# Chunked attention: softmax reciprocals transposed by TensorE, returned through DRAM and applied by GpSimd, and row statistics placed after three projections

## The chip, the cores and the metric

The kernel runs on one core of one Trainium2 chip. The metric is the device time of one execution in microseconds (us); the median of several executions is compared. A trace of one profiled execution shows when each engine worked: TensorE (PE, with its weight loads PEld), VectorE (DVE), ScalarE (ACT), GpSimd (POOL), and SyncE (SP), whose queue issues most DMA transfers.

## The reference

Two layers over 1024 tokens of width 1024: an even one (two recurrent head groups) and an odd one (softmax attention of 64-token chunks), each followed by a squared-ReLU MLP and a gated embedding. The change lies in the odd layer's attention: 16 heads of width 64, each chunk against itself and the eight chunks before it.

```python
def rmsnorm(x, g, eps=NORM_EPS):
    xf = x.astype(jnp.float32)
    y = xf * lax.rsqrt(jnp.mean(xf * xf, -1, keepdims=True) + eps)
    return (y * g.astype(jnp.float32)).astype(x.dtype)
...
def chunk_band_attention(h, w_qkv, q_g, k_g, rel_bias):
    qkv = (h @ w_qkv).reshape(bsz, seq, 3, C_HEADS, C_HEAD_DIM)
    q = rmsnorm(qkv[:, :, 0], q_g) * (C_HEAD_DIM ** -0.5)
    k = rmsnorm(qkv[:, :, 1], k_g)
    v = qkv[:, :, 2]
...
        s = jnp.einsum('bqhd,bkhd->bhqk', q_c, k_b).astype(jnp.float32) + bias
        s = jnp.where(valid, s, -jnp.inf)
        prob = jax.nn.softmax(s, -1).astype(v.dtype)
        return jnp.einsum('bhqk,bkhd->bqhd', prob, v_b)
...
        h = rmsnorm(x, norm_mix_g[i])
            mix = chunk_band_attention(h, attn_w_qkv[o], attn_q_g[o], attn_k_g[o], attn_rel_bias[o]) @ attn_w_out[o]
        x = x + mix
```

## The kernel before

The program is generated for one core. Activations lie transposed (128 features by 1024 tokens, in two halves `hf` of 512). Float32 products are made of two-part splits: a rounded high part and the remainder, three matmuls for each product (`xh*wh`, `xh*wl`, `xl*wh`). All matmuls are issued by the helper `mm` (L177), all transposes by TensorE by `tr` (L192), and most splits by `split_scaled` (L349 on ScalarE, L350 on VectorE); so these lines of the profile hold many tiles, and the tile names tell them apart.

**Steps.** Attention runs over 16 steps `s`: 8 pairs of heads (`pr`) times 2 halves of the tokens (`hf`). Four kinds of generators ("lanes") write the instructions down, and `run` (L130) merges them by a planner's clock: each `yield` names a duration in the table `LAT` after which the lane may go on, or a mark of another lane that it has to see first.

- `attn_in` (L1828) projects q, k and v of one step: four blocks `i` of 128 tokens, 24 matmuls each, into a PSUM bank `dps` (two banks in turn, `bank`). ScalarE evicts with the row statistics `rscol` as a scale (L1861 to `qk`, L1865 to `vs`), VectorE writes the remainder (L1866). GpSimd squares q and k (L1873, tile `sq`), VectorE sums the squares (L1874, `ss`), takes a reciprocal root and scales `qk` (L1877). The lane may be three steps ahead of attention. In the first block (L1858) `row_stats` (L366) sums the squares of layer 0's output over the features with matmuls against ones, and VectorE makes `rscol` of them. Those squares are summed by GpSimd while layer 0 ends (L1627, tile `acc`).
- `attn_norm` (L1880) transposes q and k on TensorE and splits them (tiles `F`, `Ql`).
- `attn_lane` (L1807), two of them, takes the 64 jobs (step, head, half of the half) in turn and runs `attn_block` (L1907). A job has two rows of 128 queries. Scores go to the banks `sn` (the last three key blocks, which have a bias) and `sf` (the far ones); VectorE adds the bias `toep` and takes the maximum (L1957, L1965); ScalarE takes the exponential and the row sums (L1967, L1970), VectorE adds the sums and takes the reciprocal (L1972, L1973), and ScalarE scales the whole row of probabilities `pb` by it (L1974). Then TensorE transposes the probabilities (bank `pt`, two in turn), they are split to `ptile` (L349, L350), and TensorE multiplies them with the values into the bank `po`. When both halves are done, ScalarE and VectorE add the two parts to `y` (L2015, L2016), and SP stores `y` to DRAM (L2022, `yd`). The last step keeps `y` on the chip.

After the last step of `attn_ins`, the same lane projects the layer's embedding (L1650, with sums of squares on GpSimd at L1675) and begins the output projection (`out_early`, L1679), which reads `yd` back.

**What sets the order.** Beyond the lanes, a scheduler orders the instructions that are ready, engine by engine. Each engine executes its list strictly in order: what stands behind a waiting instruction waits too. SP's list has the loads of weights (L1823), of biases (L1841) and the stores of `y`.

Of the kernel before, what the change touches and what calls it, by code (L numbers as in the profile page):

```python
# [8 lines left out]
F32 = mybir.dt.float32  # L9
# [76 lines left out]
    "attn_block0": 0.97,  # L86
    "attn_block1": 4.45,
    "attn_block2": 0.43,
    "attn_block3": 0.94,
    "qk": 11.25,  # L90
    "norm": 1.28,
# [18 lines left out]
class Trunk:  # L110
# [254 lines left out]

    def row_stats(self, accs, out, scale=1.0 / D, eps=1e-6):  # L366

        nc = self.nc
        nt = out.shape[-1]
        ps = self.stat_bank()  # L370
        for i in range(nt):
            self.mm(ps[:, i:i + 1], accs[i // 4][:, (i % 4) * P:(i % 4 + 1) * P], self.ones[:, 0:1],
                             start=True, stop=True)
        ms = self.sm.tile([P, NT], F32, tag="ms", name="ms")[:, 0:nt]
        nc.vector.tensor_scalar(ms, ps[:, 0:nt], scale, eps, op0=ALU.mult, op1=ALU.add)
        self.rsqrt_small(out, ms, [P, nt], "n")
# [1361 lines left out]
    def layer1_in(self):  # L1738
        nc, tc, a = self.nc, self.tc, self.a
        with ExitStack() as es:  # L1740
# [15 lines left out]
            jobs = iter([(s, h, b) for s in range(16) for h in range(2) for b in range(2)])  # L1756
            self.run([self.attn_lane(steps, jobs, l1, rbl) for _ in range(2)] + [self.attn_norms(steps, l1), self.attn_ins(steps, l1)])

    def attn_ins(self, steps, l1):
# [27 lines left out]
        def xt():  # L1787
            n = q["n"] = q.get("n", -1) + 1
            if n % 4 == 0:
                q["x"] = act([P, 4, HB], F32)  # L1790
            return q["x"][:, n % 4, :]
        yield from self.out_early(1, self.xd, lambda q: act([P, 2, 2, HB], F32R), xt, load_w,
                                  [("at", 14), ("at", 14), ("at", 14), ("at", 15)])

# [12 lines left out]
    def attn_lane(self, steps, jobs, l1, rbl):  # L1807

        for s, h, b in jobs:
            yield ("in", s)  # L1810
            yield from self.attn_block(s, *steps[s], h, b, l1, rbl)

    def weights3(self, odd):
# [14 lines left out]
    def attn_in(self, pr, hf, l1, kv):  # L1828
# [16 lines left out]
        vs = l1.tile([P, 4, 2, P], F32R, tag="vs", name="vs", bufs=4)  # L1845
        kv["vs"] = kv["vs"] + [vs]
        for e in range(4):
            i = 4 * hf + e
            ps = self.bank([P, 3, P])
            ts = slice(i * P, i * P + P)  # L1850
            for k in range(NK):
# [5 lines left out]
                yield 0  # L1857
            if pr == 0 and i == 0:  # L1858
                self.row_stats(self.accs, self.rscol)
            rc = self.rscol[:, i:i + 1]  # L1860
            A.activation(qk[:, e, :], ps[:, 0:2, :].rearrange("p a c -> p (a c)"), AF.Copy, scale=rc)  # L1861
            v3 = ps[:, 2, :].rearrange("p (h d) -> p h d", h=2)
            vf = vs[:, e].rearrange("p h c -> p (h c)").rearrange("p (q d) -> p q d", d=64)
            hi = vf[:, 0:4:3, :]
            A.activation(hi, v3, AF.Copy, scale=rc)  # L1865
            V.scalar_tensor_tensor(vf[:, 1:3, :], v3, rc, hi.bitcast(F32), op0=ALU.mult, op1=ALU.subtract)  # L1866
            yield 0
# [39 lines left out]
    def attn_block(self, s, pr, hf, h, blk, l1, rbl):  # L1907
# [36 lines left out]
        for j, (b, o, c0, c1) in place.items():  # L1944
            used[b] = max(used[b], o + c1 - c0)
        probs = []
        for m in (m0, m0 + 1):
            n0 = max(0, m - 2)
# [22 lines left out]
            if nf:  # L1971
                V.tensor_tensor(l[:, 0:1], l[:, 0:1], l[:, 1:2], op=ALU.add)  # L1972
            V.reciprocal(l[:, 2:3], l[:, 0:1])  # L1973
            A.activation(pb[:, 0:(nf + nn) * P], pb[:, 0:(nf + nn) * P], AF.Copy, scale=l[:, 2:3])  # L1974
            probs.append((pb, f0))
# [33 lines left out]
        if blk == 1:  # L2009
            if h == 0:  # L2010
                st["y"] = l1.tile([P, HB], F32, tag="y", name="y", bufs=1)
            y, po = st["y"], st["po", h]
# [4 lines left out]
            if h == 1:  # L2017
                if s == 15:
                    yield ("ylast", 0)
                    self.split_scaled(self.ylast, y, None, slice(0, HB))  # L2020
                else:
                    nc.sync.dma_start(out=self.yd[pr][hf], in_=y)  # L2022
# [94 lines left out]
```

## Time and profile before

| | |
|---|---|
| median of three runs | 3090.18 us (3086.09 to 3090.59) |
| profiled execution | 3089.73 us, of which the span of its instructions is 3088.0 us |
| mean granted TensorE clock | 0.978 |
| start of layer 1's projections | 1680.72 us |
| stores of `y` of steps 0 and 14 | 1767.81 and 2252.96 us |
| removed line L1974 | 128 instructions, 86.2 us of ScalarE |

The profile has a page (busy time by engine, the span in 40 slices, the chain of work that ended last, groups of instructions by line) and answers on the trace: the timeline, waits, groups, and busy time by stretch. In a row, `out<-in` names the tiles without their numbers, then the shape, the count `xN`, busy time and mean duration; "idle before" is the time for which the engine stood before these instructions, with what ended it.

### The profile page before, as it was taken

To read this page: it belongs to the slowest core of one execution; us is meant where nothing else is said; L and a number is where in the kernel's file an instruction comes from. 1 tells how busy PE (TensorE), PEld (TensorE's weight loads), DVE (VectorE), ACT (ScalarE), POOL (GpSimd) and SP (SyncE) were. 2 spreads that over 40 slices of the span, in tenths; PEclk is the share of its full clock that TensorE was granted. 3 is DMA by queue.
4 is the path that set the end of the run, shared out by engine and by line. 5 is a ranking of instruction groups with operands and counts; after the bars stand their busy time and mean duration, and the time that the engine had idled before them with its cause. 6 is when DMAs were issued, how large, how long until landed. Compare 5 with 4: busy or idle time off the path is not lost.

```text
span 3088.0 us, 47130 instructions
## 1 busy us (share of the span) xinstructions
PE 2979.5 (96%) x17288; PEld 2461.2 (80%) x17288; DVE 2232.1 (72%) x4518; ACT 1510.7 (49%) x2922; POOL 544.9 (18%) x978
## 2 busy tenths in 40 slices
PE   7999999999999999999999999989899999999999
PEld 5777778777777888888887988888788888888887
DVE  6656676657849788878867666766768888888762
ACT  4333443334427544444434577777756544544431
POOL 6533442443500000000015111100110000000002
PEclk9999999999999999999999999999999999999999
DMA  4211112211346434754424101100256444754432
GB/s 138 72 54 62 55 55 74 62 53 64 125 158 219 158 148 150 259 167 150 137 89 144 34 33 36 53 33 16 72 177 225 151 154 150 255 172 150 126 109 102
DMA packets 187639, 358.45 MB, mean 116 GB/s; under 512 B 45712, under 2 KB 47888, under 8 KB 187408
## 3 DMA queue, kind: packets, MB, share of 16 engines
q1 hardware_dynamic: 158608, 303.00, 29.6%
q10 hardware_dynamic: 28800, 52.44, 4.4%
q8 instruction: 136, 2.23, 0.3%
q14 instruction: 95, 0.78, 0.1%
HBM read 262.04 MB, written 93.32 MB: 115 GB/s over the span
## 4 chain that ended last, share of the span: by engine, by line
PE 79%; DVE 10%; ACT 4%; DMA 3%; POOL 2%; issue 2%; SPq 0%; DVEq 0%; POOLq 0%; ACTq 0%
PE dps L177 66%; PE ch L177 2%; PE pm L177 2%; PE iz L177 1%; PE po L177 1%; PE tp L177 1%; DVE ptile L350 1%; PE pt L192 1%; DVE pb L1957 1%; PE sn L177 1%; POOL subt L415 1%; PE py L177 1%; DMA wraw<-in_w_qkv 1%; ACT pb L1970 1%; POOL sub L417 1%
## 5 line engine op out<-in xcount | busy, mean ns | idle before, releaser
L177 PE MATMUL dps<-r,act 128*128 128x512 f32 x3528 | 829.4, 392 | 0.0
L177 PEld LDWEIGHTS dps<-r,act 128*128 128x128 f32 x3528 | 662.0, 188 | 145.8
L177 PE MATMUL dps<-xg,whi 128*128 128x512 f32 x1280 | 434.0, 419 | 14.9 <-ACT xg L352 7.4
L1614 POOL TENSOR_TENSOR pn<-pn,prs 128x512 f32<-128x512 f32 x32 | 47.1, 1474 | 1543.1 <-ACT prs L386 1447.7
L177 PE MATMUL dps<-wq,act 128*128 128x384 f32 x1536 | 305.7, 345 | 6.4 <-DVE vs L1866 3.1
L177 PEld LDWEIGHTS dps<-xg,whi 128*128 128x128 f32 x1280 | 233.9, 195 | 67.9 <-issue 8.0
L177 PEld LDWEIGHTS dps<-wq,act 128*128 128x128 f32 x1536 | 266.6, 191 | 10.5 <-DVE vs L1866 4.9
L177 PE MATMUL dps<-xg,wlo 128*128 128x512 f32 x640 | 258.8, 405 | 1.3 <-DVE wlo L304 1.3
L177 PE MATMUL dps<-late,act 128*128 128x512 f32 x960 | 229.2, 392 | 0.0
L177 PEld LDWEIGHTS dps<-late,act 128*128 128x128 f32 x960 | 180.3, 188 | 39.7
L1271 ACT CAST act<-act 128x512 fp32r<-128x512 f32 (+1 forms) x223 | 137.6, 649 | 131.6 <-PE dps L177 67.5
L1384 DVE TENSOR_TENSOR late<-late,dps 128x512 f32<-128x512 f32 x224 | 152.4, 684 | 52.2 <-PE dps L177 45.8
L1271 ACT CAST act<-late 128x512 fp32r<-128x512 f32 x210 | 124.2, 617 | 133.2 <-PE dps L177 90.4
L177 PE MATMUL dps<-act 128*128 128x512 f32 x672 | 165.0, 392 | 0.0
L1272 DVE TENSOR_TENSOR act<-act 128x512 fp32r<-128x512 f32 (+1 forms) x223 | 154.8, 721 | 6.0 <-ACT act L1271 5.8
L177 PEld LDWEIGHTS dps<-act 128*128 128x128 f32 x672 | 126.1, 188 | 28.7
L1272 DVE TENSOR_TENSOR act<-late,act 128x512 fp32r<-128x512 f32 x210 | 141.5, 688 | 8.9 <-ACT act L1271 7.0
L177 PEld LDWEIGHTS dps<-xg,wlo 128*128 128x128 f32 x640 | 124.4, 194 | 29.2 <-DVE wlo L304 1.8
L303 ACT CAST whi<-wraw 128x1024 fp32r<-128x1024 f32 x78 | 81.9, 1050 | 122.0 <-PE dps L177 82.4
L1522 DVE TENSOR_TENSOR xw<-xw,dps 128x512 f32<-128x512 f32 x174 | 118.0, 683 | 31.5 <-PE dps L177 31.5
L177 PE MATMUL dps<-xw,act 128*128 128x512 f32 x576 | 139.6, 392 | 0.0
L1389 ACT ACTIVATE late<-late 128x512 f32<-128x512 f32 x128 | 80.3, 630 | 119.4 <-DVE late L1384 113.5
(484 smaller groups left out, 5656.7 us busy)
## 6 DMA issues: line engine op xcount, KB each, us to landing
hb<-late ACTq DMA_DIRECT2D x168, 256.0 KB
act<-hb SPq DMA_DIRECT2D x138, 256.0 KB
late<-in_w SPq DMA_DIRECT2D x60, 512.0 KB
wraw<-in_w_in SPq DMA_DIRECT2D x56, 512.0 KB
act<-in_w SPq DMA_DIRECT2D x96, 256.0 KB
braw<-hb SPq DMA_DIRECT2D x72, 256.0 KB
wraw<-in_w_out SPq DMA_DIRECT2D x21, 512.0 KB
wraw<-in_w_qkv SPq DMA_DIRECT2D x21, 512.0 KB
```

What stands on the lines that cost most here:

```text
L177: return self.begin(self.nc.tensor.matmul(out, lhsT, rhs, start=start, stop=stop, skip_group_check=again))
L192: return self.begin(self.nc.tensor.transpose(out, in_, ident))
L303: nc.scalar.copy(hi, raw)
L350: nc.vector.tensor_tensor(dst[:, 1, sl], src, dst[:, 0, sl].bitcast(F32), op=ALU.subtract)
L415: E.tensor_tensor(o, X[:, 0:i, i:i + 1].broadcast_to((NP, i, n)), Bq[:, i:i + 1, i + 1:16].broadcast_to((NP, i, n)), op=ALU.mult)
L417: E.tensor_tensor(X[:, 0:i, i + 1:16], X[:, 0:i, i + 1:16], o, op=ALU.add)
L1271: A.copy(hi, s)
L1272: V.tensor_tensor(lo, s, hi.bitcast(F32), op=ALU.subtract)
L1384: V.tensor_tensor(r, t, u, op=ALU.add)
L1389: A.activation(t, t, AF.Relu)
L1522: V.tensor_tensor(x[n][:, hs[hf]], x[n][:, hs[hf]], ps, op=ALU.add)
L1614: G.tensor_tensor(pn, pn, prs[:, sl], op=ALU.mult)
```

## The change

Steps 0 to 13 no longer scale the probabilities; the product with the values is made of the unscaled ones. The reciprocals of a step are collected in a tile `rl` (128 queries by 2 heads by 4 rows). A new lane `attn_sums` waits until a step's `y` is whole, transposes `rl` to 8 by 128 on TensorE (into a `pt` bank), copies it to `rt` on ScalarE, stores it to DRAM (`rd`), loads it back twice so that each reciprocal is repeated over the 64 partitions of its head (`R`), multiplies `y` by `R` on GpSimd and stores `y`. Steps 14 and 15 scale as before. `y` has two buffers instead of one. The first two blocks of the first projection go to the `sn` banks, and the row statistics are taken when the third block is written; the three blocks are evicted together after that. In the output projection two marks change from `at` to `sums`, and the table of durations gets three rows and one new number.

```diff
@@ -84,9 +84,12 @@
     "gdn_back4": 1.83,
     "attn_norm0": 0.24,
     "attn_block0": 0.97,
-    "attn_block1": 4.45,
+    "attn_block1": 3.70,
     "attn_block2": 0.43,
     "attn_block3": 0.94,
+    "attn_sums0": 0.60,
+    "attn_sums1": 6.00,
+    "attn_sums2": 8.00,
     "qk": 11.25,
     "norm": 1.28,
     "end_front": 46.33,
@@ -363,11 +366,11 @@
             nc.scalar.activation(sq, src, AF.Square)
             nc.gpsimd.tensor_tensor(acc, acc, sq, op=ALU.add)
 
-    def row_stats(self, accs, out, scale=1.0 / D, eps=1e-6):
+    def row_stats(self, accs, out, scale=1.0 / D, eps=1e-6, bank=None):
 
         nc = self.nc
         nt = out.shape[-1]
-        ps = self.stat_bank()
+        ps = bank if bank is not None else self.stat_bank()
         for i in range(nt):
             self.mm(ps[:, i:i + 1], accs[i // 4][:, (i % 4) * P:(i % 4 + 1) * P], self.ones[:, 0:1],
                              start=True, stop=True)
@@ -1754,7 +1757,7 @@
             self.ql = [[pool.tile([P, HB], F32R, tag=tag, name="Ql", bufs=1) for pool, tag in
                         ((self.accp, f"acc{e}"), (l1, f"Ql{e}"))] for e in range(2)]
             jobs = iter([(s, h, b) for s in range(16) for h in range(2) for b in range(2)])
-            self.run([self.attn_lane(steps, jobs, l1, rbl) for _ in range(2)] + [self.attn_norms(steps, l1), self.attn_ins(steps, l1)])
+            self.run([self.attn_lane(steps, jobs, l1, rbl) for _ in range(2)] + [self.attn_sums(steps, l1)] + [self.attn_norms(steps, l1), self.attn_ins(steps, l1)])
 
     def attn_ins(self, steps, l1):
         kv = {}
@@ -1790,7 +1793,7 @@
                 q["x"] = act([P, 4, HB], F32)
             return q["x"][:, n % 4, :]
         yield from self.out_early(1, self.xd, lambda q: act([P, 2, 2, HB], F32R), xt, load_w,
-                                  [("at", 14), ("at", 14), ("at", 14), ("at", 15)])
+                                  [("sums", 14), ("sums", 14), ("at", 14), ("at", 15)])
 
     def attn_norms(self, steps, l1):
         K = []
@@ -1809,6 +1812,28 @@
         for s, h, b in jobs:
             yield ("in", s)
             yield from self.attn_block(s, *steps[s], h, b, l1, rbl)
+
+    def attn_sums(self, steps, l1):
+
+        nc = self.nc
+        for s, (pr, hf) in enumerate(steps[:14]):
+            yield ("at", s)
+            rd = self.dr.tile([1, T], F32, tag="rd", name="rd", bufs=2)
+            pt = self.psm.tile([P, HB], F32, tag="pt", name="pt", bufs=2)[0:8, 0:P]
+            self.tr(pt, self.st[s]["rl"].rearrange("p h m -> p (h m)"), self.ident)
+            rt = self.sm.tile([8, P], F32, tag="rt", name="rt")
+            nc.scalar.copy(rt, pt)
+            yield "attn_sums0"
+            nc.sync.dma_start(out=rd.rearrange("o (m q) -> (o m) q", m=8), in_=rt)
+            yield "attn_sums1"
+            R, y = l1.tile([P, HB], F32, tag="R", name="R", bufs=1), self.st[s]["y"]
+            for h in range(2):
+                nc.sync.dma_start(out=R[64 * h:64 * h + 64], in_=rd[:, h * HB:h * HB + HB].broadcast_to((64, HB)))
+            yield "attn_sums2"
+            nc.gpsimd.tensor_tensor(y, y, R, op=ALU.mult)
+            nc.sync.dma_start(out=self.yd[pr][hf], in_=y)
+        yield ("at", 14)
+        self.mark(("sums", 14))
 
     def weights3(self, odd):
 
@@ -1844,9 +1869,21 @@
         qk = wp.tile([P, 4, 256], F32, tag="qk", name="qk")
         vs = l1.tile([P, 4, 2, P], F32R, tag="vs", name="vs", bufs=4)
         kv["vs"] = kv["vs"] + [vs]
+        def scale(i, e, ps):
+            rc = self.rscol[:, i:i + 1]
+            A.activation(qk[:, e, :], ps[:, 0:2, :].rearrange("p a c -> p (a c)"), AF.Copy, scale=rc)
+            v3 = ps[:, 2, :].rearrange("p (h d) -> p h d", h=2)
+            vf = vs[:, e].rearrange("p h c -> p (h c)").rearrange("p (q d) -> p q d", d=64)
+            hi = vf[:, 0:4:3, :]
+            A.activation(hi, v3, AF.Copy, scale=rc)
+            V.scalar_tensor_tensor(vf[:, 1:3, :], v3, rc, hi.bitcast(F32), op0=ALU.mult, op1=ALU.subtract)
+        held = []
         for e in range(4):
             i = 4 * hf + e
-            ps = self.bank([P, 3, P])
+            if pr == 0 and i < 2:
+                ps = psm.tile([P, HB], F32, tag="sn", name="dps", bufs=2)[:, 0:3 * P].rearrange("p (a c) -> p a c", a=3)
+            else:
+                ps = self.bank([P, 3, P])
             ts = slice(i * P, i * P + P)
             for k in range(NK):
                 ks = slice(k * P, k * P + P)
@@ -1855,15 +1892,13 @@
                 self.mm(ps, xh, wl[:, :, ks], start=False, stop=False)
                 self.mm(ps, xl, wh[:, :, ks], start=False, stop=k == NK - 1)
                 yield 0
-            if pr == 0 and i == 0:
-                self.row_stats(self.accs, self.rscol)
-            rc = self.rscol[:, i:i + 1]
-            A.activation(qk[:, e, :], ps[:, 0:2, :].rearrange("p a c -> p (a c)"), AF.Copy, scale=rc)
-            v3 = ps[:, 2, :].rearrange("p (h d) -> p h d", h=2)
-            vf = vs[:, e].rearrange("p h c -> p (h c)").rearrange("p (q d) -> p q d", d=64)
-            hi = vf[:, 0:4:3, :]
-            A.activation(hi, v3, AF.Copy, scale=rc)
-            V.scalar_tensor_tensor(vf[:, 1:3, :], v3, rc, hi.bitcast(F32), op0=ALU.mult, op1=ALU.subtract)
+            held.append((i, e, ps))
+            if pr == 0 and i == 2:
+                self.row_stats(self.accs, self.rscol, bank=psm.tile([P, HB], F32, tag="pt", name="st", bufs=2))
+            if pr or i > 1:
+                for h in held:
+                    scale(*h)
+                held.clear()
             yield 0
         q4 = qk.rearrange("p i c -> p (i c)").rearrange("p (n d) -> p n d", d=64)
         ss = self.sm.tile([P, 16], F32, tag="ss1", name="ss1")
@@ -1944,6 +1979,8 @@
         for j, (b, o, c0, c1) in place.items():
             used[b] = max(used[b], o + c1 - c0)
         probs = []
+        if h == 0 and blk == 0:
+            st["rl"] = sm.tile([P, 2, 4], F32, tag="rl", name="rl", bufs=4)
         for m in (m0, m0 + 1):
             n0 = max(0, m - 2)
             nn = m - n0 + 1
@@ -1970,8 +2007,10 @@
             A.activation(S, S, AF.Exp, bias=mx[:, 2:3], accum_out=l[:, 0:1])
             if nf:
                 V.tensor_tensor(l[:, 0:1], l[:, 0:1], l[:, 1:2], op=ALU.add)
-            V.reciprocal(l[:, 2:3], l[:, 0:1])
-            A.activation(pb[:, 0:(nf + nn) * P], pb[:, 0:(nf + nn) * P], AF.Copy, scale=l[:, 2:3])
+            rl = st["rl"][:, h, m % 4:m % 4 + 1]
+            V.reciprocal(rl, l[:, 0:1])
+            if s > 13:
+                A.activation(pb[:, 0:(nf + nn) * P], pb[:, 0:(nf + nn) * P], AF.Copy, scale=rl)
             probs.append((pb, f0))
             yield "attn_block0"
         yield "attn_block1"
@@ -2008,7 +2047,7 @@
                 q += 1
         if blk == 1:
             if h == 0:
-                st["y"] = l1.tile([P, HB], F32, tag="y", name="y", bufs=1)
+                st["y"] = l1.tile([P, HB], F32, tag="y", name="y", bufs=2)
             y, po = st["y"], st["po", h]
             oth = slice(64 * (1 - h), 64 * (1 - h) + 64)
             tmp = l1.tile([P, HB], F32, tag="otmp", name="otmp", bufs=1)
@@ -2018,7 +2057,7 @@
                 if s == 15:
                     yield ("ylast", 0)
                     self.split_scaled(self.ylast, y, None, slice(0, HB))
-                else:
+                elif s == 14:
                     nc.sync.dma_start(out=self.yd[pr][hf], in_=y)
                 self.dump("y1", y, (pr, slice(None), slice(hf * HB, hf * HB + HB)))
                 self.mark(("at", s))
```

The first place is TensorE at the start of layer 1. Here the rows carry numbers, since the bank tells the blocks apart: before, `dps_15881` is the first block's bank and `dps_15906` holds the statistics (`ones`, `acc`).

```order
L177 MATMUL dps_15881<-wq0_15743,act_15785 128x384
L177 MATMUL dps_15881<-wq1_15744,act_15785 128x384
L177 MATMUL dps_15881<-wq0_15743,act_15785 128x384
L177 MATMUL dps_15906<-ones_67,acc_15211 128x1 x4
L177 MATMUL dps_15906<-ones_67,acc_15212 128x1 x4
L177 MATMUL dps_15931<-wq0_15743,act_15261 128x384
L177 MATMUL dps_15931<-wq1_15744,act_15261 128x384
L177 MATMUL dps_15931<-wq0_15743,act_15261 128x384
```

After, `dps_15881` and `dps_15906` are the first and second blocks, `dps_15931` is the third (its first 23 matmuls stand ahead of the first block's), `st_15956` holds the statistics, and `dps_15987` is the fourth block.

```order
L180 MATMUL dps_15906<-wq0_15743,act_15703 128x384
L180 MATMUL dps_15906<-wq0_15743,act_15785 128x384
L180 MATMUL dps_15906<-wq1_15744,act_15785 128x384
L180 MATMUL dps_15906<-wq0_15743,act_15785 128x384
L180 MATMUL dps_15931<-wq0_15743,act_15785 128x384
L180 MATMUL st_15956<-ones_67,acc_15211 128x1 x4
L180 MATMUL st_15956<-ones_67,acc_15212 128x1 x4
L180 MATMUL dps_15987<-wq0_15743,act_15261 128x384
L180 MATMUL dps_15987<-wq1_15744,act_15261 128x384
```

The statistics have moved from behind the 24th matmul of projection to behind the 72nd.

The second place is ScalarE where an odd step's last job meets the next step's first ones. Before:

```order
L1967 ACTIVATE pb,l<-sf,mx 128x256
L1970 ACTIVATE pb,l<-pb,mx 128x384
L1970 ACTIVATE pb,l<-pb,mx 128x128
L1970 ACTIVATE pb,l<-pb,mx 128x256
L1974 ACTIVATE pb<-pb,l 128x640
L1974 ACTIVATE pb<-pb,l 128x128
L1974 ACTIVATE pb<-pb,l 128x256
L349 CAST ptile<-pt 128x512 x2
L349 CAST ptile<-pt 128x256
```

After:

```order
L2004 ACTIVATE pb,l<-sf,mx 128x256
L2007 ACTIVATE pb,l<-pb,mx 128x384
L2007 ACTIVATE pb,l<-pb,mx 128x128
L2007 ACTIVATE pb,l<-pb,mx 128x256
L352 CAST ptile<-pt 128x512 x2
L352 CAST ptile<-pt 128x256
L1825 COPY rt<-pt 8x128
L2007 ACTIVATE pb,l<-pb,mx 128x384
```

Three rows of scaling between the exponentials and the casts of the transposed probabilities are gone, and the copy of the transposed sums stands behind the casts.

The third place is GpSimd in the middle of attention, where it squares q and k (`sq`) and prepares the biases (`toep`). Before:

```order
L1873 TENSOR_TENSOR sq<-qk 128x512 x2
L1915 TENSOR_SCALAR toep<-toep,rbl 128x384
L1916 MEMSET toep 64x64
L1873 TENSOR_TENSOR sq<-qk 128x512 x2
L1915 TENSOR_SCALAR toep<-toep,rbl 128x384
L1916 MEMSET toep 64x64
```

After:

```order
L1908 TENSOR_TENSOR sq<-qk 128x512
L1950 TENSOR_SCALAR toep<-toep,rbl 128x384
L1951 MEMSET toep 64x64
L1908 TENSOR_TENSOR sq<-qk 128x512 x2
L1833 TENSOR_TENSOR y<-y,R 128x512
L1908 TENSOR_TENSOR sq<-qk 128x512
L1833 TENSOR_TENSOR y<-y,R 128x512
L1950 TENSOR_SCALAR toep<-toep,rbl 128x384
L1951 MEMSET toep 64x64
```

A multiply by the returned reciprocals stands before the second square of a step and another behind it, ahead of the next bias.

## The prediction

> **What bounds the kernel now.** I read the page first: the span and the busy shares.
>
> ```profile
> span 3088.0 us, 47130 instructions
> PE 2979.5 (96%) x17288; PEld 2461.2 (80%) x17288; DVE 2232.1 (72%) x4518; ACT 1510.7 (49%) x2922; POOL 544.9 (18%) x978
> ```
>
> TensorE (PE) is busy for 2979.5 of 3088.0 us, so the kernel can only win what PE idles (108.5 us) and what it loses to a lowered clock. Next I cut out attention, which the timeline puts at about 1720 to 2300 us. The columns are PE, weight loads, VectorE (DVE), ScalarE (ACT), GpSimd (POOL), granted clock, DMA share and GB/s.
>
> ```profile
> 1720.00:2300.00 580.00, 532.51 (x3292) 493.08 (x3290) 411.35 (x1314) 423.88 (x988) 70.99 (x70) 0.97 0.17 56
> ```
>
> PE idles 580.00 - 532.51 = 47.5 us here, and a mean clock of 0.97 is worth another 0.03 x 580 = 17 us at most. The view of waits, for PE from 1720 to 2310 us, says what ended that idle time (total, times, longest):
>
> ```profile
> PE pt L192 <- ACT pb L1974: 8.4, 9, 1.8
> PE po L177 <- ACT ptile L349: 6.6, 14, 1.0
> PE po L177 <- DVE ptile L350: 6.1, 11, 1.4
> PE sf L177 <- ACT pb L1967: 4.0, 7, 1.5
> ```
>
> The first row is the instruction that the change removes: the scaling of the probabilities by 1/sum, which the transposes (pt) wait for. The chain of waits in the same stretch gives that line 2.3% of 590 us, 13.6 us:
>
> ```profile
> by line: PE dps L177 41.7%; PE po L177 5.0%; DVE ptile L350 5.0%; PE pt L192 4.9%; DVE pb L1957 3.8%; PE sn L177 3.8%; ACT pb L1970 3.2%; issue 2.8%; DMA wraw<-in_w_qkv 2.6%; ACT pb L1974 2.3%; DVE F L1902 2.3%; PE sf L177 2.2%; ACT ptile L
> ```
>
> **The change, part by part.** *Three projections ahead of the statistics.* The timeline of the start of layer 1 (start, duration, and in brackets PE's idle time and what ended it), with the GpSimd and VectorE rows that it hangs on:
>
> ```profile
> 1684.87 0.62 PE L177 MATMUL dps<-wq,act 128*128 128x384 f32 x2 [0.32 <-ACT act L352]
> 1685.81 0.45 PE L177 MATMUL dps<-wq,act 128*128 128x384 f32 x1 [0.32 <-DVE act L353]
> 1686.93 1.05 PE L177 MATMUL dps<-ones,acc 128*128 128x1 f32 x8 [0.68 <-POOL acc L1627]
> 1692.09 1.86 PE L177 MATMUL dps<-ones,acc 128*128 128x1 f32 x8 [4.11 <-POOL acc L1627]
> 1694.60 27.96 PE L177 MATMUL dps<-wq,act 128*128 128x384 f32 x144 [0.64 <-DVE ms L375]
> 1722.39 0.60 PE L192 MATMUL dps<-ident,qk 128*128 128x128 f32 x4
> ```
>
> ```profile
> 1690.78 1.26 POOL L1627 TENSOR_TENSOR acc<-acc,late 128x512 f32<-128x512 f32 x1
> 1694.38 0.16 DVE L375 TENSOR_SCALAR ms<-dps 128x8 f32<-128x8 f32 x1
> 1696.59 0.17 DVE L291 SCALAR_TENSOR_TENSOR rscol<-rsw,rscol 128x8 f32<-128x8 f32 x1
> 1705.95 0.47 ACT L1861 ACTIVATE qk<-dps,rscol 128x256 f32<-128x256 f32 x1 [3.42 <-PE dps L177]
> 1718.43 0.47 ACT L1861 ACTIVATE qk<-dps,rscol 128x256 f32<-128x256 f32 x1 [3.42 <-PE dps L177]
> ```
>
> PE stands 0.68 + 4.11 + 0.64 = 5.4 us for sums that GpSimd delivers at 1692.04. It then runs at half clock:
>
> ```profile
> 1688.00:1692.00 4.00, 0.00 (x0) 0.00 (x0) 1.31 (x3) 2.29 (x3) 3.79 (x4) 0.79 0.93 352
> 1692.00:1696.00 4.00, 3.27 (x12) 3.18 (x13) 3.64 (x10) 1.05 (x1) 3.29 (x6) 0.50 0.45 153
> 1696.00:1700.00 4.00, 4.00 (x14) 4.00 (x14) 2.14 (x6) 1.68 (x3) 0.30 (x2) 0.50 0.39 135
> ...
> 1748.00:1752.00 4.00, 2.65 (x19) 2.18 (x17) 3.90 (x12) 3.89 (x10) 0.00 (x0) 0.97 0.00 0
> 1752.00:1756.00 4.00, 4.00 (x17) 3.94 (x17) 3.65 (x13) 3.88 (x9) 0.00 (x0) 0.60 0.02 4
> 1872.00:1876.00 4.00, 2.40 (x13) 1.97 (x14) 2.06 (x6) 2.93 (x8) 0.00 (x0) 0.83 0.00 0
> 1876.00:1880.00 4.00, 4.00 (x24) 3.69 (x23) 2.93 (x17) 2.96 (x10) 0.00 (x0) 0.74 0.00 0
> ```
>
> A projection block of 24 matmuls takes (1718.43 - 1705.95)/3 = 4.16 us at full clock. After the change the first 23 matmuls (up to the pair at 1684.87) stand where they stood; then come 48 + 1 more in place of the wait, ending at about 1685.2 + 49/24 x 4.16 = 1693.7. The sums are there by then (1692.04). The 16 statistics matmuls cost 2 x 1.05 = 2.1 us, to 1695.8, and block four runs to 1700.0. Block five needs the bank of block three, which waits for the statistics: before, 1694.38 - 1693.95 = 0.4 us to VectorE's first and 2.4 us to its last instruction, so 1698.6; then three evictions of some 0.8 us (an L1861 of 0.47 and its successor) and VectorE's half, about 1702. **This new wait is 2 us.** Blocks five to seven end at 1702 + 12.5 = 1714.5 in place of 1722.39. I take **-8 us**; the ends are -5.4 (idle time alone) and -9.9 (no new wait).
>
> *The scaling on ScalarE.* It goes from steps 0 to 13, that is from 112 of 128 blocks. The group of all, and the largest form:
>
> ```profile
> L1974 ACT ACTIVATE pb<-pb,l 128x640 f32<-128x640 f32 (+4 forms) x128 | 86.2, 694 | 18.4 <-DVE l L1973 15.5 <-DVE ss L1875 1.6 <-DVE rsw L290 0.9
> ```
>
> 112 x 0.694 = 77.7 us leave an engine that is busy 423.88 of 580 us. That engine is not the bound, so only the stretches count in which PE waits. One of them, where a step turns:
>
> ```profile
> 2010.64 0.19 ACT L1970 ACTIVATION_READ_ACCUMULATOR pb<-pb,mx 128x1 f32 x1
> 2010.73 1.51 ACT L1974 ACTIVATE pb<-pb,l 128x640 f32<-128x640 f32 x3
> ...
> 2011.60 0.88 PE L192 MATMUL pt<-ident,pb 128*128 128x128 f32 x6 [1.75 <-ACT pb L1974]
> ```
>
> The transposes could begin when the exponential of their block is done, and the casts L349 follow 1.5 us sooner. What is late next is that exponential (L1970, 3.2% of the chain). The bounds: 0 if it takes the whole place; 8.4 + 6.6 + 6.1 + 4.0 = 25.1 us if every wait named above goes. I take **-13 us**, nearest to the chain's 13.6.
>
> *The clock.* The four rows above at 1748 and 1872 show a lowered clock after stretches where PE was busy 2.4 to 2.7 of 4 us. The mean of 0.97 is worth up to 17 us; with 13 of 47.5 us of idle time gone I take a like share, **-4 us** (0 to -17).
> [...]
>
> *Transposing the sums.* 14 transposes to 8 x 128, each with a ScalarE copy. The nearest PE rows:
>
> ```profile
> L192 PE MATMUL dps<-ident,f 8*128 8x8 f32 x8 | 1.0, 231 | 8.8 <-DVE f L714 8.8
> PE pt L192 <- DVE ptile L350: 4.0, 9, 0.9
> ```
>
> Six in a row took 0.88 us above, 0.147 each; a lone one 0.231, and one that waits for a pt bank 4.0/9 = 0.44 more. So 2.1 to 9.4 us; I take **+2.5**. The copies, at the 0.47 us of an L1861 some 6.6 us in all, lie inside the 77.7 us freed.
>
> *Through DRAM and back, GpSimd's multiply.* Per step three loads and stores on SP's queue, then one multiply. An issue on SP, the nearest round trip in layer 0's chain, the nearest multiply, and a square with its reader:
>
> ```profile
> 2155.91 0.33 SPq L2022 DMA_DIRECT2D yd<-y  x1
> ```
>
> ```profile
> 341.73 1.61 DMA z<-sub
> 343.41 1.95 DMA Xp<-z
> ```
>
> ```profile
> L1627 POOL TENSOR_TENSOR acc<-acc,late x14: 1261/1595/2279, 1616.4 to 1690.8; 128x512 f32<-128x512 f32 x14
> ```
>
> ```profile
> 2063.73 1.04 POOL L1873 TENSOR_TENSOR sq<-qk 128x512 f32<-128x512 f32 x1 [16.51 <-ACT qk L1861]
> ...
> 2066.74 0.68 DVE L1874 TENSOR_REDUCE ss<-sq 128x8 f32<-128x512 f32 x1
> ```
>
> 56 issues of 0.33 us are 18 us of SP's 580, 14 of them (yd) there before. From the copy to the end of the multiply: 3 x 0.33 + 1.61 + 1.95 + 1.26 = 5.8 us. GpSimd is busy 71 of 580 us, so the multiply itself is covered; but it stands in GpSimd's order between two squares (sq), VectorE's sum of squares (L1874) waits for the square, and everything on VectorE waits behind that. The square is done 66.74 - 64.77 = 2.0 us ahead of its reader. The hold is 0 where the factors land early, and 5.8 - 2.0 = 3.8 us a step, 53 us in all, where the square's input is ready as the copy starts. GpSimd had idled 16.51 us before the square shown, so there is mostly room for a multiply; I take the near end, **+2 us**, with the 1.6 us that step 13's multiply adds among the embedding's sums.
>
> The sum: -8 - 13 - 4 + 2.5 + 2 = -20.5. The profiled execution took 3089.73 us for its span of 3088.0, and the median of the three runs is 3090.18, so it stands for them. 3089.7 - 20.5 = **3069 us**.
>
> **Rivals.** *VectorE is held by GpSimd* (slower). Place: L1874 behind a multiply that waits for its factors. For it speaks that the round trip is longer than the 2.0 us of slack; against it, that GpSimd idles long before a square. The other terms give -22.5, so it decides from 1.6 us a step; at 3 us a step it is 42 - 22.5 = +19.5, 3109 us.
> [...]
>
> ```profile
> L1825 DVE TENSOR_TENSOR wq<-wraw,wq x21: 1204/1223/1523, 1691.6 to 2071.9; 128x1024 fp32r<-128x1024 f32 x21
> L1825 DVE TENSOR_TENSOR wq<-late,wq x3: 1430/2196/2307, 1668.0 to 1675.2; 128x1024 fp32r<-128x1024 f32 x3
> ```
>
> The three beside GpSimd's L1627 took 2.20 against 1.22 us; 14 such meetings are 13.6 us of VectorE, and if all lay on the path, 3083, inside the next case.
>
> *The gain is hidden*: the exponential and VectorE's casts are late in place of the scaling, and the clock stays. Then only the start is left: -8 + 4.5 = 3086. For it: DVE ptile has 5.0% of the chain, more than twice the removed line.
>
> *The clock does not move*: all else as forecast, 3073; it speaks for this that dips follow turns of a step, which stay.
>
> *PE's idle time goes almost whole*: -9 - 25 - 12 + 4 = -42, 3048. For it: three of the four largest waits end on ScalarE.
>
> **How the numbers follow.** Forecast, 3060 to 3078 with the unmoved clock in it: 0.45. Idle time gone, 3040 to 3060: 0.17. Hidden, 3078 to 3096: 0.23, half of it below 3084. Slower, above 3096: 0.15. The range 3046 to 3097 leaves out the lowest 0.05 and the slower 0.15. About 0.2% (6 us) is what a measurement of this kernel can tell from no change, so faster is below 3084.0: 0.45 + 0.17 + 0.12 = 0.74; same 0.11; slower 0.15.
>
> **What would show it.** At the start: no PE wait for the sums, full clock from 1685 to 1714, and a wait of about 2 us for the eviction of block three. In attention: no wait of pt on ScalarE over 1 us, PE idle near 34 us in place of 47.5, clock 0.98. At the new part: a group "sum of squares waits for square" of a few us; tens would be the slower rival. I am wrong at the root if ScalarE loses its 78 us and PE's idle time stays.

## The result and the profile after

The changed kernel takes 3083.22 us (median of 10 runs, 3077.51 to 3089.14); the kernel before took 3091.66 us beside it (10 runs, 3086.09 to 3096.97). The ratio is 0.997, with a 95% interval of 0.9959 to 0.9981: **9 us faster by the ratio (8.4 between the medians), where 20.5 were forecast.** The profiled execution took 3083.45 us. The page's head:

```profile
span 3081.7 us, 47201 instructions
PE 2969.4 (96%) x17302; PEld 2463.0 (80%) x17302; DVE 2233.0 (72%) x4518; ACT 1444.9 (47%) x2824; POOL 562.3 (18%) x992
```

ScalarE lost 65.8 us net (1510.7 before). TensorE is busy for 10.1 us less; its idle time did not fall (112.3 us, 108.5 before). So the parts have to be read apart.

**The start of layer 1.** PE's timeline (start, duration, idle time and what ended it), then ScalarE's and VectorE's rows of the same stretch:

```profile
1683.04 3.83 PE L180 MATMUL dps<-wq,act 128*128 128x384 f32 x21
1688.57 9.11 PE L180 MATMUL dps<-wq,act 128*128 128x384 f32 x51 [1.70 <-ACT act L355]
1697.52 1.84 PE L180 MATMUL st<-ones,acc 128*128 128x1 f32 x16
1699.22 4.41 PE L180 MATMUL dps<-wq,act 128*128 128x384 f32 x24
1707.91 15.53 PE L180 MATMUL dps<-wq,act 128*128 128x384 f32 x72 [4.27 <-DVE vs L1879]
1723.27 0.60 PE L195 MATMUL dps<-ident,qk 128*128 128x128 f32 x4
...
1701.01 1.05 ACT L1849 CAST wq<-wraw 128x1024 fp32r<-128x1024 f32 x1 [3.53 <-DMA wraw<-in_w_qkv]
1702.09 1.22 DVE L1850 TENSOR_TENSOR wq<-wraw,wq 128x1024 fp32r<-128x1024 f32 x1 [3.36 <-ACT wq L1849]
1703.23 0.16 DVE L378 TENSOR_SCALAR ms<-st 128x8 f32<-128x8 f32 x1
1707.50 0.35 DVE L1879 SCALAR_TENSOR_TENSOR vs<-dps,rscol,vs 128x128 fp32r<-128x128 f32 x1 [0.27 <-ACT vs L1878]
```

The wait for GpSimd's sums is gone, as forecast: the statistics matmuls (st) follow three blocks without a gap. But their first VectorE instruction (ms) begins at 1703.23, 3.87 us after they end at 1699.36. VectorE stood idle for 2.73 us of that, up to 1702.09: ahead of ms in its order stands the remainder (L1850) of the third weight tile of the *next* head pair, which waits for ScalarE's cast, which waits for the load. Before, ms (at 1694.38) stood ahead of that remainder:

```profile
1697.67 1.23 DVE L1825 TENSOR_TENSOR wq<-wraw,wq 128x1024 fp32r<-128x1024 f32 x1 [0.92 <-ACT wq L1824]
```

So after the change PE waits 4.27 us for the eviction of block three, and the clock falls, as the windows show (PE's busy time comes second, the granted clock third from the end):

```profile
1700.00:1704.00 4.00, 3.63 (x21) 3.31 (x20) 1.80 (x5) 1.05 (x1) 1.03 (x3) 1.00 0.48 158
1704.00:1708.00 4.00, 0.09 (x1) 0.09 (x1) 2.36 (x11) 2.51 (x8) 1.04 (x1) 0.89 0.45 133
1708.00:1712.00 4.00, 4.00 (x13) 4.00 (x14) 2.77 (x11) 0.09 (x1) 1.04 (x1) 0.50 0.01 2
1712.00:1716.00 4.00, 4.00 (x20) 4.00 (x19) 0.32 (x3) 0.73 (x2) 0.00 (x0) 0.76 0.00 0
```

From the layer's first projection to the last it took 1723.27 - 1683.04 = 40.2 us, and 1722.39 - 1680.72 = 41.7 before: 1.4 us won of 8.

**The steps.** From there to the first product of the layer's tail (the first matmul that reads `late`), the kernel before and then the changed one:

```profile
1722.39:2330.12 607.73, 560.24 (x3417) 515.51 (x3416) 422.54 (x1329) 434.14 (x1002) 70.96 (x69) 0.97 0.19 63
```

```profile
1723.27:2323.00 599.73, 555.37 (x3432) 520.08 (x3430) 429.53 (x1332) 369.94 (x908) 90.67 (x83) 0.97 0.22 72
```

8.0 us less, with idle time of 44.4 (before 47.5) and the clock as low as before. The view of waits, PE from 1700 or 1720 to 2310 us, names another engine now: VectorE's remainders of the transposed probabilities (ptile).

```profile
PE pt L195 <- DVE ptile L353: 9.3, 12, 1.5
PE po L180 <- DVE ptile L353: 4.0, 7, 0.9
PE dps L180 <- DVE F L1937: 4.0, 5, 1.2
...
PE pt L195 <- ACT pb L2013: 2.0, 1, 2.0
```

The scaling keeps one wait, of 2.0 us, in a step that still scales. The new part's groups are small; here they are, with what VectorE's sum of squares waits for behind the multiply:

```profile
L1833 POOL TENSOR_TENSOR y<-y,R x14: 1272/1284/1298, 1769.8 to 2218.1; 128x512 f32<-128x512 f32 x14
L195 PE MATMUL pt<-ident,rl 128*8 128x128 f32 x14 | 4.2, 302 | 0.0
...
L1909 DVE TENSOR_REDUCE ss<-sq x32: 621/677/687, 1707.8 to 2196.5; 128x8 f32<-128x512 f32 x32
its engine sat idle before it (us, times) until:
  POOL sq L1908: 2.5, 4
```

**The tail.** A wait that nobody forecast:

```profile
2309.84 10.66 PE L180 MATMUL dps<-act,wq 128*128 128x512 f32 x45
2319.75 2.51 DVE L1275 TENSOR_TENSOR late<-late 128x1024 fp32r<-128x1024 f32 x2 [8.49 <-ACT late L1274]
2322.17 0.68 DVE L1301 TENSOR_TENSOR late<-late,dps 128x512 f32<-128x512 f32 x1
2323.00 9.34 PE L180 MATMUL dps<-act,late 128*128 128x512 f32 x39 [2.50 <-ACT r L1274]
```

PE's wait is put down to a cast, but it starts 0.15 us after the end (2322.85) of L1301, which empties the PSUM bank that held the output projection's first block. The tail's banks go round in a ring with one counter (`bank()`); the three tiles that the start no longer takes from it (two blocks in `sn`, the statistics in `pt`) shift the ring, and the tail begins on a bank that is still full. Before, the next bank was free: PE began the tail at 2330.12 without a wait, 1.21 us ahead of the same instruction (L1298 there).

### The profile page after: what moved, and what is told of

Same layout as the page of the kernel before. It is cut to its first block, busy times and chain, and to the rows that moved or that the text cites. A ratio compares the mean times of both kernels' runs of the same rounds, so it can differ in the third digit from the quotient of the medians.

```text
span 3081.7 us, 47201 instructions
## 1 busy us (share of the span) xinstructions
PE 2969.4 (96%) x17302; PEld 2463.0 (80%) x17302; DVE 2233.0 (72%) x4518; ACT 1444.9 (47%) x2824; POOL 562.3 (18%) x992
## 4 chain that ended last, share of the span: by engine, by line
PE 80%; DVE 9%; ACT 4%; DMA 3%; POOL 2%; issue 2%; SPq 0%; DVEq 0%; ACTq 0%; POOLq 0%
PE dps L180 66%; PE ch L180 2%; PE po L180 2%; PE pm L180 2%; PE pt L195 1%; PE iz L180 1%; PE sn L180 1%; PE tp L180 1%; DMA wraw<-in_w_qkv 1%; PE py L180 1%; POOL sub L420 1%; POOL subt L418 1%; PE pp L180 1%; DVE ptile L353 1%; DMA act<-in_w 1%
```

## The experiments

Layer 0, which the change does not touch, ends anywhere from 1678.3 to 1692.3 us from execution to execution, and from the tail's first product to the end all take 757.9 to 758.7 us. So besides the ratio of the timed runs I compare one stretch of the traces: from the first projection of layer 1 to the first product of its tail, in two pieces that meet at the first transpose of `qk`. Several numbers stand for several executions.

| kernel | to last projection | steps, to the tail | sum | ratio to before (95%) |
|---|---|---|---|---|
| before | 41.7, 42.0 | 607.7, 605.9 | 649.4, 647.9 | 1 |
| changed | 40.2, 39.5, 38.8 | 599.7, 595.8, 596.2 | 640.0, 635.3, 635.0 | 0.997 (0.9959-0.9981) |
| e1 start alone | 37.9 | 605.2 | 643.1 | 0.9975 (0.9965-0.9986) |
| e2 sums alone | 41.9, 41.8 | 595.3, 595.5 | 637.2, 637.2 | 0.9958 (0.9946-0.997) |
| e3 ring mended | 38.4 | 596.8 | 635.2 | 0.9949 (0.9932-0.9965) |
| e4 order mended | 33.4 | 595.4 | 628.9 | 0.9934 (0.9923-0.9946) |
| e5 both mended | 32.8 | 595.2 | 628.0 | 0.9923 (0.991-0.9937) |
| e6 e5, scaling kept | 33.0 | 618.6 | 651.6 | 1.0014 (1.0003-1.0025) |
| e7 e5, no lane of sums | 33.8 | 592.8 | 626.6 | 0.992 (0.9907-0.9934) |
| e8 e5, remainders on GpSimd | 33.7 | 608.8 | 642.5 | 0.9968 (0.9955-0.998) |
| e9 e5, number 4.45 | 33.7 | 598.6 | 632.3 | 0.9938 (0.9919-0.9958) |
| e10 e6, number 4.45 | 33.5 | 613.1 | 646.5 | 0.9995 (0.9981-1.0009) |
| e11 start alone, mended | 33.3 | 600.9 | 634.2 | 0.9958 (0.9945-0.9971) |
| e12 e5, number 3.20 | 32.8 | 614.3 | 647.0 | 0.9995 (0.9983-1.0007) |

**Each part alone.** e1 is the kernel before with the edits of `attn_in` and `row_stats`; e2 has all the rest.

> The kernel before with the three projections ahead of the statistics alone; the scaling stays on ScalarE, no sums are transposed. Prediction on record for this part: -8 us against before, blocks 5 to 7 done 7.9 us earlier after the start of layer 1. Theory A (VectorE's order): the statistics stand behind the remainder of the third weight tile of the next head pair, which waits for its load, so PE waits about 4 us for the eviction of block three and then runs at a lowered clock: the stretch from the start of layer 1 to the last projection is about 40.3 us (41.7 before), -1.4 us. Theory B (the ring of PSUM banks): the part takes three tiles fewer from the ring, so that layer 1's tail begins on a bank that still holds the output projection's first block, and PE waits about 2.5 us there. A and B together: -1.4 + 2.5 = +1 us against before; A alone -1.4; neither -8.

> The changed kernel with the start of layer 1 as it was before: only the softmax sums' part of the change. Prediction on record for this part: -13 - 4 + 2.5 + 2 = -12.5 us against before. Theory B (ring of banks): this kernel has before's ring, so no wait of PE at the begin of the tail; its gain is what the steps' stretch showed, about -14, less the 4 us of projection matmuls that the steps' waits took before and that now stand behind the last step: -9 to -11 us. Rival, that the wait at the tail belongs to the attention's earlier end (weights late): the 2.5 us wait is there and the gain is -7 to -8 us.

e2 met the forecast of its part: 637.2 against a mean of 648.7 before, -11.4 (forecast -12.5), with no wait at the tail. e1 has theory A's wait (4.20 us for the eviction of block three); at the tail it waits only 0.64 us, and the stretch is 5.6 us shorter, more than A and B gave and less than the forecast. Its start takes 37.9 us, less than the changed kernel's, as the record of the clock has one window of half clock there, where the changed kernel has two. The timed ratio of e1 is worth 7.7 us, and its interval (4 to 11 us) includes the forecast of 8. Together the parts should give -17; the changed kernel gives -9 to -14.

**The ring** (e3) and **the order on VectorE** (e4), each on the changed kernel. In e4, `ev3` is the last cast of the three held blocks' evictions; the edge holds back ScalarE's cast of the weight tile, and VectorE's remainder, which reads that cast, comes later with it.

```diff
             if pr == 0 and i == 2:
+                self.nd += 3
                 self.row_stats(
```

```diff
-            nc.scalar.copy(wh[:, j, :], raw)
+            c = nc.scalar.copy(wh[:, j, :], raw)
+            if pr == 1 and j == 2:
+                edge = mybir.DependencyInfo(mybir.DependencyClass.NoSync, mybir.DependencyReason.DATA)
+                self.tc.add_manual_dep(c.ins, self.ev3.ins.name, edge, reason="order")
```

> The changed kernel with the counter of the PSUM ring moved on by three where the start no longer takes from it, so that the tail's first products get banks 2 and 7 as before, in place of banks 1 and 0. Theory B: the wait of 2.50 us of PE at the begin of the tail goes or falls under 0.5 us; 2 to 3 us faster than the changed kernel (3080 to 3081 where that has 3083). Rival (the weights of the tail arrive late, the bank has no part in it): the wait stays at 2.5 us and the time does not move.

> The changed kernel with the cast and the remainder of the third weight tile of the next head pair ordered behind the evictions of blocks one to three. Theory A: the statistics begin on VectorE within 0.5 us of the statistics matmuls' end, the wait for the eviction of block three falls from 4.27 us to under 2 us, PE's clock stays at full from there, and the seventh block ends 4 to 7 us earlier after the start of layer 1; the time falls by as much. Rival (the sums of GpSimd or the statistics chain itself are the limit): the wait stays over 3 us. A second rival: the weights of the next head pair come later by this and the first steps of attention wait instead; then the stretch to the last projection is shorter and the time does not move.

PE's row at the tail of e3 has no wait:

```profile
2316.28 28.63 PE L180 MATMUL dps<-act,late 128*128 128x512 f32 x122
```

L1301 ends there at 2316.77, after the tail has begun on another bank. That confirms whose wait it was. Its size was not 2.5 us in general: in two more executions of the changed kernel (below) it was 0.60 and 0.18, each time ending 0.15 us after L1301, and these two took the 635 us of e3. e3's interval overlaps the changed kernel's, so a gain beyond the wait is not shown.

e4 is the main result. VectorE, PE and a window of its start:

```profile
1701.95 0.17 DVE L378 TENSOR_SCALAR ms<-st 128x8 f32<-128x8 f32 x1 [1.54 <-PE st L180]
1706.65 12.75 PE L180 MATMUL dps<-wq,act 128*128 128x384 f32 x72 [0.46 <-DVE vs L1882]
```

```profile
1708.00:1712.00 4.00, 4.00 (x25) 4.00 (x24) 3.02 (x13) 0.73 (x2) 1.30 (x1) 1.00 0.37 133
```

The statistics begin 0.04 us after their matmuls, the wait is 0.46 us, the clock stays full, and the 72 matmuls take 12.75 us in place of 15.53. The start takes 33.4 us, where the forecast had 33.8 (1714.5 - 1680.72). The stretch is 628.9, 6 to 11 us shorter than the changed kernel's, and the intervals of the timed ratios do not overlap. The steps take 595.4 us, no more than in the changed kernel, so they do not wait for the later weights.

**Both mends** (e5).

> Both mends together: the ring's counter moved on by three, and the third weight tile ordered behind the evictions. From the start of layer 1 to the end, the changed kernel took 1398.7 us, the ring alone 1393.6, the order alone 1387.6 with 1.18 us of the tail's wait left. Theory (two separate causes, A and B): 1386 to 1387, no wait of PE at the begin of the tail, ratio to before 0.993. Rival (one cause, and the earlier end only moves the wait to the weights of the tail): 1388, as the order alone, with a wait of 1 us or more at the tail.

628.0, with no wait at the tail, and 1386.5 to the end, as the theory had it; the 1.1 us to e4 is less than executions of one kernel differ by, so only the missing wait speaks for two causes. The ratio says 0.9923. This kernel beats both others: 3072.73 us median where the kernel before took 3093.35 beside it.

**What the scaling and the new lane are worth**, on e5. e6 scales all steps (`if s > 13` becomes `if True`), e7 drops `attn_sums` and stores `y` as before, e9 and e10 set the planner's number back (`"attn_block1": 4.45`) in e5 and e6, and e12 sets it to 3.20.

> As the kernel with both mends, but ScalarE scales the probabilities of all 16 steps as before and GpSimd scales the finished steps as well, so the factor is applied twice in steps 0 to 13. The difference to the kernel with both mends is what the scaling's removal is worth by itself. Prediction on record: -13 for the scaling and -4 for the clock, so this is 17 us slower than the kernel with both mends, with waits of the transposes for the scaling of 8 us in all back in the trace. Rival (the gain is hidden, VectorE is late in its place): within 3 us.

> As the kernel with both mends, but without the lane of the sums: no transposes of the sums, no trip through DRAM, no multiply on GpSimd; steps 0 to 13 are stored without their normalisation, and the output projection may start at the end of step 14 as before. The difference to the kernel with both mends is the price of the new part. Prediction on record: +2.5 for the transposes and +2 for the trip and the multiply, so this is 4 to 5 us faster. Rival (GpSimd's multiply holds VectorE): over 10 us faster. Third case: below 2 us, the part costs next to nothing.

> As the kernel with both mends, but with the planner's number for the end of an attention block (attn_block1) at 4.45 us as before, in place of 3.70. From the start of layer 1 to the first product of its tail the kernel with both mends took 628.0 us, with the scaling kept on ScalarE 651.6. Theory (the planner's number carries part of the gain): 4 to 10 us slower than with 3.70, since transposes and second products then stand later than the data. Rival (the engine's work alone matters): within 2 us.

> As the kernel with both mends, but the probabilities of all steps are scaled on ScalarE as before (the factor is applied twice in steps 0 to 13) and attn_block1 is 4.45. Theory: keeping the scaling cost 23.6 us because the order written for 3.70 us asks for the transposes before the scaling is done; with before's number it costs 12 to 16 us against the kernel with both mends (640 to 644 us of layer 1 ahead of its tail), about what the prediction gave for scaling and clock together (17). Rival (the number plays no part): again 650 to 653 us.

> As the kernel with both mends, with attn_block1 at 3.20 us in place of 3.70. If the planner's number still stands too long for the shorter chain: 2 to 5 us faster than 628.0 us ahead of the tail. If 3.70 fits the chain as it is: slower by 2 to 10 us, since the transposes are asked for before the exponential is done.

PE's waits in e6, in e10, and in e12:

```profile
PE pt L195 <- ACT pb L2020: 16.4, 11, 2.8
```

```profile
PE pt L195 <- ACT pb L2020: 8.1, 10, 1.7
```

```profile
PE po L180 <- ACT ptile L352: 17.9, 17, 1.8
```

Keeping the scaling costs 23.6 us in the order written for 3.70 (e6 - e5, where 17 were expected), and 14.3 in the order written for 4.45 (e10 - e9). The clean price is the second (17.6 us by the timed ratios): e9 and e10 have 12 windows of half clock each between the last projection and the tail, while e6 has 13 to e5's 8, and e10 shows the same 8 us of waits for the scaling as the kernel before. e10's 646.5 is 18.5 above e5 and misses its expectation of 640 to 644, which left out what e9 costs by itself. That is 4.3 us in e9 against e5 (4.6 by the ratios, whose intervals overlap), but 0.9 of it stands at the start, which the number doesn't touch, and in the steps PE idles less in e9 (42.0 us) than in e5 (44.3); what is left lies in the clock's 12 windows against 8. Executions of one kernel differ by as many (below), so it is not shown that 3.70 is better than 4.45. 3.20 costs 19, twice the most that was expected and far outside the intervals: the products with the values (po) are then asked for before ScalarE has cast their operand. The new lane costs 628.0 - 626.6 = 1.4 us, the third case of e7; that is no more than executions of one kernel differ by, and the intervals of the ratios nearly coincide.

**VectorE relieved** (e8): the remainders of the later weight tiles on GpSimd.

```diff
-            nc.vector.tensor_tensor(wl[:, j, :], raw, wh[:, j, :].bitcast(F32), op=ALU.subtract)
+            (nc.gpsimd if pr > 1 else nc.vector).tensor_tensor(wl[:, j, :], ...)
```

> As the kernel with both mends, but the remainders of the weight tiles of head pairs 2 to 7 (18 of 1.22 us on VectorE) are taken on GpSimd. Theory: with the scaling gone VectorE is what TensorE waits for in attention (the transposes wait 9.3 us for its casts of the probabilities, the largest row), so taking 22 us off VectorE gives 3 to 8 us, and the row of transposes waiting for VectorE shrinks by half. Rival: GpSimd needs about 2.5 us for each and slows VectorE's two-input instructions beside it; the time stays within 2 us or rises.

My theory failed, 14.5 us the wrong way. The row of transposes waiting for VectorE did halve, but another grew from 4.1 to 14.1:

```profile
PE po L180 <- ACT ptile L352: 14.1, 14, 1.8
PE pt L195 <- DVE ptile L353: 4.5, 8, 1.5
L1853 POOL TENSOR_TENSOR wq<-wraw,wq x18: 2382/2426/3425, 1727.6 to 2075.1; 128x1024 fp32r<-128x1024 f32 x18
```

GpSimd takes 2.43 us for each. VectorE's ptile kept its length beside it (594 ns on the mean in both), but the two short instructions behind the sum of squares did not:

```profile
1727.62 4.81 POOL L1853 TENSOR_TENSOR wq<-wraw,wq 128x1024 fp32r<-128x1024 f32 x2 [0.15 <-ACT wq L1849]
1728.22 1.86 DVE L1917 TENSOR_SCALAR ss<-ss 128x16 f32<-128x16 f32 x1
1730.12 2.34 DVE L289 TENSOR_SCALAR nn<-ss 128x16 int32<-128x16 int32 x1
1733.89 0.30 PE L180 MATMUL sn<-F,Ql 128*128 128x128 f32 x1 [2.07 <-DVE rsw L292]
```

The second ends at 1732.46, 0.03 us after GpSimd's pair. Of the 30 such instructions behind the first transposes, nine that lay beside GpSimd's remainders took 0.67 to 4.04 us in place of 0.17, 17 us more in all; in e5 none took over 0.22. So VectorE lost most of the 21.9 us that the move took off it, and the rival was right that VectorE is slower beside GpSimd here, though these instructions read one tile and not two. How much of the 14.5 us comes by this way is not separated: the casts on ScalarE come late, as in e12, and by which link of the order is open.

**The start as it was drawn** (e11): e1 with both mends.

> The kernel before with the start part alone and both mends (ring counter, third weight tile behind the evictions): the start part as the prediction drew it, with nothing in its way. Prediction on record: -8. From the start of layer 1 to the last projection 33 to 34 us in place of 41.7, 8 us less; if the earlier start passes to the end, 640 to 642 us ahead of the tail where before took 649.4 and the start part without mends 643.1. Rival (attention is bound elsewhere and the earlier start only makes the steps wait): 643 or more.

33.3 us at the start and 634.2 in all: 8 us at the start, as the forecast drew it, and 14.5 in the whole stretch (13.0 by the ratio), better than either expectation. Why the steps behind it got 6 us shorter as well is open; beside the sums' part the mended start gives less, 9.2 (e5 against e2).

**The same kernels again**, untouched, to see what one execution is worth.

> The changed kernel as it is, another execution. If the lowered clock belongs to the kernel: again 11 to 13 windows of half clock (3.4 us each) between the last projection and the first product of the tail, and 638 to 642 us from the start of layer 1 to there. If it is chance of the one execution: 8 to 10 windows and 633 to 637 us.

> The changed kernel as it is, a third execution, with the same two expectations as the second. Two that agree with each other and differ from the first speak for chance in the first.

> The kernel before as it is, another execution: 9 windows and 649.4 us in the first. If executions scatter by chance, by some 3 us either way here too; if not, within 1 us.

> The sums part alone, another execution: 8 windows and 637.2 us in the first. If executions scatter by chance, by some 3 us either way; if not, within 1 us, and the sums part alone stays ahead of the whole change by about 3 us.

The changed kernel took 635.3 and 635.0 where the first execution took 640.0, with 8 and 10 windows of half clock, counted in the trace's record of the clock, between the last projection and the tail where the first had 12. So 5 us of the first trace belong to that execution and not to the kernel, about 2 of them in the tail's wait. The kernel before came out at 647.9, the sums alone at 637.2 once more, so it is not ahead of the whole change by the 3 us that its expectation had.

## Why the forecast was wrong, step by step

- *Three projections ahead* (-8). **This is the step that failed.** Right: the sums' wait goes, and blocks one to three fill it. Wrong: "before, 1694.38 - 1693.95 = 0.4 us to VectorE's first" was carried over as if VectorE were free whenever the statistics come. VectorE took its list in the order written; with the statistics later, the third weight remainder of the next head pair stands ahead of them and waits for a load (it ended at 1703.31, the statistics' matmuls at 1699.36). The new wait was 4.27 us, not 2 (4.28 and 4.53 in the other two executions), and cost 6.83 us of half clock as well; in the nine kernels with the order mended it is 0.46 to 0.79 us, so the forecast's 2 us fit neither case. Beside the sums' part the edit brought 637.2 - 635.1 = 2 us in two executions and a loss of 3 in one; the timed ratios put the whole change (0.997) behind the sums alone (0.9958), with overlapping intervals. With order and ring mended (e5 against e2) it brings 9.2.
- *The ring of banks* was not in the forecast. It cost 0.2 to 2.5 us.
- *Scaling and clock* (-13 - 4). e10 against e9 gives 14.3, and it is the scaling's alone, since the clock's windows are as many in both. The term for the clock did not come: 9 and 8 windows of half clock in the steps before, 12, 8 and 10 in the changed kernel. The mechanism was ScalarE's line ahead of the transposes, as forecast (PE waited 8.4 us for it before, 2.0 us after). But PE's idle time in the steps fell to 44.4, 44.5 and 43.2 us, not to 34: the waits went to VectorE's ptile, the engine that "the gain is hidden" named, and the time came out of PE's busy part, which fell by 4.9 to 9.0 us with 14 matmuls more. The matmuls themselves did not get shorter: in e2, where PE's busy part is 8.2 us less, their durations add up to 1113.7 us, and to 1113.6 before. Their records overlap more, as PE breaks off in 72 places in place of 103; that each break costs busy time too is the likely reason, but no run tests it.
- *Transposes* (+2.5), *trip and multiply* (+2): 1.4 together. The trip was longer than the estimate of 5.8 us; one step's rows on ScalarE, SP and GpSimd:

```profile
1946.28 0.25 ACT L1825 COPY rt<-pt 8x128 f32<-8x128 f32 x1 [0.49 <-PE pt L195]
1947.80 1.09 SPq L1831 DMA_DIRECT2D R<-rd  x2
1952.71 1.27 POOL L1833 TENSOR_TENSOR y<-y,R 128x512 f32<-128x512 f32 x1 [7.96 <-DMA R<-rd]
```

  From 1946.53 to 1953.98 it is 7.45 us, and it is hidden: VectorE's sum of squares waited for the square 2.5 us in all 16 steps (1.6 before), so the slower rival did not come. The multiply did hold five of VectorE's short instructions in the steps, 4.1 us beyond their usual lengths in all, where the forecast had 13.6 at most. (The three rows from which it took that price lasted 1.43, 2.31 and 2.20 us, and the second lay beside another GpSimd instruction, L1614, and not L1627.)

With nothing in the start's way the whole gives 628.0 - 648.7 = -20.7 us (e5), for a forecast of -20.5; part of that agreement is luck, since the scaling gave 2.7 less than its two terms, the new part cost 3.1 less, and the start gave 1.2 more. The changed kernel lacks what VectorE's order takes: -9 to -14 in the traces, -9 in the timed runs.

## What to carry to other kernels

When an edit moves an instruction later on a busy engine, list what the engine's order now puts ahead of it, and follow each of those to its last input: a load for work far ahead can sit in front of a result that is needed at once (here ms began 3.87 us after its matmuls, and 0.04 us after them in e4). Tiles taken from another place also shift every later round of the ring that they used to come from. A planner's number that goes with a change belongs in the forecast as a term of its own: here 0.5 us less of it cost 19 us. And work moved to an engine that idles can still hold the engine that it was taken from (nine short instructions of VectorE took 0.67 to 4.04 us in place of 0.17 in e8), so look at the lengths of short instructions beside it, and not only at the long ones.

## What the runs showed of the hardware

In these traces the clock falls in windows of 3.41 us, and by how much of one PE works, also where no single wait is long. Three windows of 3.4 us of the changed kernel, and PE's longest wait ahead of the drop:

```profile
1802.70:1806.10 3.40, 1.99 (x13) 1.54 (x14) 1.86 (x6) 2.65 (x10) 0.00 (x0) 1.00 0.00 0
1806.10:1809.50 3.40, 3.40 (x19) 3.33 (x18) 2.17 (x12) 1.74 (x6) 0.00 (x0) 0.50 0.01 1
1809.50:1812.90 3.40, 2.55 (x18) 2.24 (x18) 2.81 (x15) 3.35 (x12) 0.00 (x0) 1.00 0.26 80
```

```profile
PE pt L195 <- ACT pb L2004: 1.2, 1, 1.2
```

In the first window PE works 1.99 of 3.4 us, with no wait over 1.2 us; the second is at half clock, the third at full. I cut layer 1 of all 18 traces (1690 to 2320 us) into windows of 3.413 us, the shortest stretch of half clock in the traces of the kernel before and of the changed one, on the grid on which the clock's changes lie in each trace, and took those at full clock. Where PE was busy for less than half of one, the next was at half clock in 79 of 86 cases; from half to three quarters in 50 of 313; above in none of 2713. Every stretch of half clock in layer 1 up to its tail lasts 3.41 us or a multiple of it, in the changed kernel 6.83 us from 1707.13 and 10.24 us from 2246.44. In the three executions of the changed kernel the grid lies 0.93, 0.54 and 3.38 us behind the first transposes of `qk`, so the same waits can fall into one window in one execution and into two in another. That fits the 8 to 12 half windows of one unchanged kernel.
